# Spatial weights and six blocks of rows turned by VectorE instead of TensorE

## The chip, the core and the metric

The kernel runs on one core of a Trainium2 chip. The metric is the device time of one execution in microseconds (us). The core's engines run side by side, each through a list of instructions of its own, and wait for each other by semaphores: TensorE (PE in the profile, its weight loads PEld) multiplies and writes to PSUM; VectorE (DVE) and ScalarE (ACT) compute element by element; GpSimd (POOL) does a little arithmetic and issues transfers; SyncE (SP) issues transfers only.

## The reference

It is one inference step of a decoder layer. 256 prompt rows and 8 sample rows, each 2048 wide, all in float32, go through two sub-layers. The first has three token mixers side by side:

```python
h = rmsnorm(x, g_pre_mix) * (1.0 + sc1) + sh1          # sh, sc, gt: silu(c) @ w_ada + b_ada, in six parts
z = h @ w_in                                           # 2048 -> 15376, split into the branches' inputs
y_a = u * (einsum('gnm,bcmge->bcnge', w_s * tril, v) + b_s)   # A: spatial gating, w_s is 8 groups of 128x128
y_b, y_c = ...                                         # B: HGRN2 recurrence, C: GLA recurrence
merged = sum_n sigmoid(z_gate[n]) * (y_n @ w_branch[n])
out = merged @ w_out                                   # the output projection, 2048 -> 2048
x = x + gt1 * rmsnorm(out, g_post_mix)
h2 = rmsnorm(x, g_pre_mlp) * (1.0 + sc2) + sh2
y2 = square(relu(h2 @ w_mlp_up)) @ w_mlp_down          # 2048 -> 8192 -> 2048
x = x + gt2 * rmsnorm(y2, g_post_mlp)
```

The outputs are x for prompt and samples, the recurrent states, and the normalised v rows of the samples.

## The kernel before, in words

**Layout.** Activations lie with the features on the 128 partitions and the 264 rows (256 prompt, 8 sample) along the free axis, so that a product reads a 128x128 piece of a weight as the stationary operand and 264 columns as the moving one. A weight is loaded in float32 and split in two parts of a faster 32-bit type, `whi` (a cast by ScalarE, L673) and `wlo` (the rest, by VectorE, L677); the activations are split in the same manner, and a product is three matmuls: hi x hi, hi x lo, lo x hi.

**Granules.** The unit of work is a granule: four 128-row steps of a weight by 256 columns, which is one load of 512 KB on SP's queue, two halves to split on ScalarE and VectorE, and 24 matmuls. `Stream` loads weights five granules ahead (`LOAD_AHEAD`) and splits them two ahead (`SPLIT_AHEAD`). `linear` strings the granules of one 256-column block together (four for 2048 input rows, two for 1024) and calls `background` after each. `background` counts granules in `now`, runs what was put in `later` for an earlier count (an entry made at count n runs when `now` has passed n), and lets the generators of the mixers take steps.

**Stages.** First the input projection of the parts for branches A and B, in five chunks of the 2048 input rows (`CHUNKS`), while the first two parts of the conditioning (`First`) are made chunk by chunk; in the fourth chunk the tables for branch A are loaded (`const_a`, L907, one every other granule). Then the mixers, run as generators between granules of the remaining input projection, the gates and the branch projections; then the output projection, eight blocks of four granules; a short stage of norms; the MLP in eight slices of 1024 hidden features, each an up-projection and, one slice later, a down-projection of eight blocks of two granules; and a tail with the last norm and the residual.

**Order.** TensorE's order is the order of the code throughout. In the first stage all engines' orders are; in the mixers GpSimd's too; in the output projection and the MLP only TensorE's, while VectorE's, ScalarE's, SP's and GpSimd's orders are laid out by a planner with durations of its own. An engine waits in order: an instruction whose operand isn't there holds all behind it.

**Turning by TensorE.** A block of the output projection and of the last down-projection has features on partitions; the residual needs rows on partitions. `gated` scales a block into `g` (VectorE and ScalarE), `to_tokens` turns it by four TensorE transposes (L96), and `put_rows` (L1659, L1660) copies it out of PSUM. For the output projection `products` (L1652) and `squares` (L1656) make two sums per row, from which the next norm is known without another pass. This is done one granule after the block's end, through `later`. The spatial weights are turned by eight transposes in `mixer_a`, and masked by `triu` on their way out of PSUM.

**Turning by VectorE.** `Rows` does this elsewhere in the kernel already (v of the mixers, their keys and their outputs). `V.transpose` (L850) turns 32x32 blocks in place of one 128x128; `out` (L853) writes the 512 KB tile to DRAM (`rows_d`) on GpSimd's queue; `back` (L859) reads it again in four pieces on the same queue, so that the blocks come to their partitions; a copy puts the columns in order.

**Conditioning.** The other four of six parts are made by `Rounds`: a round is 1 MB of `w_ada` in two tiles (L379) and four matmuls of 512 columns (`ada` in the profile). A batch of rounds is due once `ADA_LAND` = 4 granules have passed since its last load. `slot` puts the mixers' small products in between granules, and counts TensorE's instructions (`T.n`) to see whether there is room for them. During the output projection six rounds of the last part are loaded ahead into spare tiles (`pre`, two at each block of `PRE_AT`). There are 28 such tiles (`blk`), shared by all stages.

Of the kernel before, what the change touches and what calls it, by code (L numbers as in the profile page):

```python
# [7 lines left out]
F32 = mybir.dt.float32  # L8
# [7 lines left out]
P = 128  # L16
# [28 lines left out]
ST_BUFS = 4  # L45
VB_BUFS = 2
N_PRE = 6
PRE_AT = (2, 3, 4)
ADA_BATCH = (4, 8)
ADA_LEAD = 3  # L50
PAIRED = 72
# [21 lines left out]
def hybrid_step_kernel(  # L73
# [288 lines left out]
    class Rounds:  # L362
# [2 lines left out]

        def __init__(self):
            self.todo, self.ws, self.done, self.at = [], [], None, 0
            self.pace, self.batch, self.gap = 5, 1, 0

        def load(self, place=None):  # L370
            r, k = self.todo.pop(0)
# [17 lines left out]

        def due(self):  # L390
            if self.ws:
                return self.full() and now[0] >= self.at + ADA_LAND
            return self.done is not None and not self.todo and now[0] >= self.at + 2 * ADA_LAND

        def tick(self):
# [435 lines left out]
        return linear(win, 0, KT, c0, width, hH, hL)  # L831


    rows_d = dp.tile([13, P, 1024], F32, tag="rows_d", name="rows_d")
    n_turned = [0]

    class Rows:
# [67 lines left out]
    def const_a(src):  # L905
        consts_a.append(blk([P, 8, P]))
        nc.sync.dma_start(consts_a[-1], src)  # L907

    srcs_a = [
        sgu_ln_g[0].partition_broadcast(P).rearrange("p (g n) -> p g n", g=8),  # L910
        sgu_ln_b[0].partition_broadcast(P).rearrange("p (g n) -> p g n", g=8),
        sgu_w_s[0].rearrange("g n m -> n g m"),
        sgu_b_s[0].rearrange("g n -> (g n)").partition_broadcast(P).rearrange("p (g n) -> p g n", g=8),
    ]
    def to_tokens(vt):
# [30 lines left out]


    def mixer_a():
        lng, lnb, wsr, bsb = consts_a
        lng, lnb = (v.rearrange("p g n -> p (g n)") for v in (lng, lnb))  # L950
        vr, vtk = rows_a.rows, []
        wsT = blk([P, 8, P])
        w00 = tmp([P, 8], "w00", 1)
        for gg in range(2):
            ps = sm()
            for i in range(4):
                T.transpose(ps[:, i * P:(i + 1) * P], wsr[:, 4 * gg + i, :], ident)
            yield
            mul(wsT[:, 4 * gg:4 * gg + 4, :], ps.rearrange("p (g n) -> p g n", g=4), triu.unsqueeze(1).to_broadcast([P, 4, P]))
        yield  # L960
        vs = tmp([P, 8, NS], "vsa", 1)
        w8 = tmp([P, 8, NS], "vsb", 1)
# [140 lines left out]
    for ci, n in enumerate(CHUNKS):  # L1103
# [5 lines left out]
        for gi in range(ng):  # L1109
# [35 lines left out]
            if final:  # L1145
                if gi in (6, 12, 18):
                    rounds.steps()
                if gi in (0, 2, 6, 8, 12, 14, 18):
                    rounds.load()
                if gi in (6, 7, 8, 9):  # L1150
                    rows_a.half((gi - 6) // 2, gi % 2)
                if gi in (8, 10):
                    rows_a.out(gi // 2 - 4)
                if gi in (11, 13):
                    rows_a.back((gi - 11) // 2)
                now[0] += 1
                if gi >= 12:
                    bg.pump(1.0)
            if ci == len(CHUNKS) - 2 and gi >= 11:
                if gi == 11:  # L1160
                    nc.sync.dma_start(cst[:, 256:904], consts[:, 256:904])
                    nc.sync.dma_start(msk, masks.rearrange("p (l t) -> p l t", l=6))
                elif gi % 2 == 0:
                    const_a(srcs_a.pop(0))
# [438 lines left out]
    branch(0, parts_a)  # L1603
    gates_b = gate_tiles(5120)
    narrow[1] = False
    branch(1, lambda: parts_b(gates_b))
    rate[:] = RATES[2]
    rounds.pace, rounds.batch, rounds.gap = 4, 4, 0
# [41 lines left out]
    def products(m, t, g, pt):  # L1650

        V.scalar_tensor_tensor(g[:, 1, 0:CW].rearrange("p (m f) -> p m f", m=2), in_rows(x1, t, m), 1.0, pt[:, t], ALU.mult, ALU.mult,  # L1652
                               accum_out=sums[:, 0, t, m:m + 1])

    def squares(m, t, g, pt):
        S.activation(g[:, 0, 0:CW].rearrange("p (m f) -> p m f", m=2), pt[:, t], AF.Square, accum_out=sums[:, 1, t, m:m + 1])  # L1656

    def put_rows(m, pt, rows):
        S.copy(in_rows(rows, 0, m), pt[:, 0])  # L1659
# [2 lines left out]
    def block_rows(m, g):  # L1662

        pt = to_tokens(g)
        for t in range(2):
            products(m, t, g, pt)
        put_rows(m, pt, og)
        for t in range(2):
            squares(m, t, g, pt)

    def norms(meanwhile):

# [12 lines left out]
    mH, mL = tiles(mh), tiles(ml)  # L1685

    sums = tmp([P, 2, 2, NS], "fs")
    pre = Rounds()
    pre.todo = [(5, k) for k in range(KT)]
    for m in range(8):  # L1690
        if m in PRE_AT:
            n = N_PRE // len(PRE_AT)
            for _ in range(n):
                pre.load(True)
        z = linear(w_out[0], 0, KT, m * CW, CW, mH, mL)
        if m < 7:
            g = gated(m, z, G1)
            later.append((now[0], lambda m=m, g=g: block_rows(m, g)))
        if m == 6:

            S.activation(tmp([P, 1], "srr", 1), sqacc[:, 0:1], AF.Sqrt)
    rounds.drain()
    rounds = pre
    A2 = A1
# [33 lines left out]
        products(7, t, g, pt)  # L1738
    both = xx3[:, 0:2]
    V.reduce_sum(both[:, :, 2:2 + NS], ps.rearrange("p s k b -> p s b k"), axis=mybir.AxisListType.X)  # L1740
    V.reduce_sum(both[:, :, 0:2], sums, axis=mybir.AxisListType.X)
    rounds.steps(3)

    d1 = tmp([P, 2, P], "vt")
# [111 lines left out]
    def down(f, ah, al):  # L1856
        for m in range(8):
# [7 lines left out]
                add(dst, dst, z)  # L1865
            if f == NFB - 1:
                g = gated(m, dst, G2)
                later.append((now[0], lambda m=m, g=g: put_rows(m, to_tokens(g), yt)))

    zs = begin_up()  # L1870
    order.__exit__(None, None, None)
# [3 lines left out]
    for f in range(NFB):  # L1875
        nxt = up(f + 1) if f + 1 < NFB else None
        if f == NFB - 1:
            rounds.drain()
            mul(G2, mod[:, 5 * KT:6 * KT, :], gpost2T.unsqueeze(2).to_broadcast([P, KT, NC]))
            yt = [[blk([P, 1024]) for _ in range(2)] for _ in range(2)]  # L1880
        last = pend
        down(f, *pend)
        pend = nxt
# [150 lines left out]
```

## Time and profile before

| | |
|---|---|
| median of 3 runs | 1782.7 us |
| the three runs | 1784.19, 1778.4, 1782.7 us |
| profiled execution | 1779.23 us |
| its span | 1777.4 us |
| TensorE matmul busy | 1756.2 us, 99% of the span, 16866 instructions |
| VectorE, ScalarE, GpSimd busy | 67%, 56%, 10% |
| granted TensorE clock, mean | 0.999 of full speed |
| moved by DMA | 455.67 MB, mean 256 GB/s |

The span goes from the first to the last instruction of the profiled execution; its own time has a little around the span. Busy shares are means over stages. The chain of waits goes back from the last instruction, at each step to what released it, so that what stands in it with its length is what set the end. In a row of the chain the first number is the start, the second the length in us; `sm L96` are transposes by TensorE, `mm L92` the products of granules, `ada L92` the conditioning. In a row of a window come its length, then busy time and count of PE, PEld, DVE, ACT and POOL, the granted clock, the mean busy share of the 16 DMA engines and GB/s.

### The profile page before, as it was taken

Reading aid. Unit: us, or ns where it says so; the run is one execution under the profiler, and the core shown is the slowest. Engines: PE = TensorE matmul, PEld = TensorE weight load, DVE = VectorE, ACT = ScalarE, POOL = GpSimd, SP = SyncE. Lnnn points to the kernel's source line nnn. Section 1 sums busy time; section 2 is a strip of 40 time slices with the busy share of each in tenths; the row PEclk is TensorE's granted clock in tenths of the full one; section 3 lists DMA queues with packets and bytes.
Section 4 is the critical chain, followed back from the end, with each engine's and each line's share of the span. In section 5 each row is a group of like instructions: output and inputs, shape, how many; then the busy total and the mean of one; then the engine's idle time right before and its main releaser. Section 6 shows DMA issues by size and latency. Waiting matters only on the chain.

```text
span 1777.4 us, 42031 instructions
## 1 busy us (share of the span) xinstructions
PE 1756.2 (99%) x16866; PEld 1675.6 (94%) x16866; DVE 1191.9 (67%) x2094; ACT 997.0 (56%) x1810; POOL 175.6 (10%) x293
## 2 busy tenths in 40 slices
PE   7999999999999999999999999999999999999998
PEld 5899999999999989899999989999999999999997
DVE  5676679887786885566666666645666666666666
ACT  5444456667777666445555666555454545454554
POOL 4222010122121122300000010000000000000000
PEclk9999999999999999999999999999999999999999
DMA  9998699899989899998667847786666666666663
GB/s 348 400 351 303 218 328 302 258 333 310 330 282 320 291 353 327 381 304 274 201 199 230 293 125 238 235 270 189 193 198 194 197 196 194 198 194 198 192 195 114
DMA packets 334547, 455.67 MB, mean 256 GB/s; under 512 B 15986, under 2 KB 277984, under 8 KB 334352
## 3 DMA queue, kind: packets, MB, share of 16 engines
q1 hardware_dynamic: 312160, 381.05, 66.3%
q0 software_dynamic: 21552, 71.48, 11.5%
q8 instruction: 132, 2.16, 0.5%
q14 instruction: 63, 0.52, 0.1%
q10 hardware_dynamic: 640, 0.47, 0.1%
HBM read 434.42 MB, written 18.51 MB: 255 GB/s over the span
## 4 chain that ended last, share of the span: by engine, by line
PE 96%; DMA 1%; DVE 1%; SPq 0%; ACT 0%; issue 0%; DVEq 0%; ACTq 0%
PE mm L92 87%; PE ada L92 5%; PE sm L92 3%; PE sm L96 1%; DMA raw<-in_w_in_dram 1%; DMA b<-in_x_prompt_dram 0%; DMA b<-in_w_ada_dram 0%; DVE wlo L677 0%; SPq L537 0%; DVE b L142 0%; DVE b L1774 0%; ACT b L148 0%; DVE b L145 0%; DVE b L139 0%; SPq L189 0%
## 5 line engine op out<-in xcount | busy, mean ns | idle before, releaser
L92 PE MATMUL mm<-b,whi 128*128 128x264 f32 x9248 | 1577.4, 277 | 1.0 <-DVE b L142 0.5
L92 PEld LDWEIGHTS mm<-b,whi 128*128 128x128 f32 x9248 | 1394.4, 189 | 34.6 <-issue 16.5
L92 PE MATMUL mm<-b,wlo 128*128 128x264 f32 x4624 | 1275.7, 276 | 0.2 <-DVE wlo L677 0.2
L677 DVE TENSOR_TENSOR wlo<-raw,whi 128x512 fp32r<-128x512 f32 x1118 | 758.4, 689 | 425.1 <-ACT whi L673 417.5
L673 ACT CAST whi<-raw 128x512 fp32r<-128x512 f32 x1118 | 679.7, 616 | 634.0 <-DVE wlo L677 320.8
L92 PEld LDWEIGHTS mm<-b,wlo 128*128 128x128 f32 x4624 | 873.5, 189 | 0.7 <-DVE wlo L677 0.4
L142 DVE TENSOR_TENSOR b<-b,mm 128x528 f32<-128x528 f32 (+1 forms) x137 | 95.7, 699 | 72.7 <-PE mm L92 66.3
L1964 POOL TENSOR_TENSOR gs<-b,G 128x16 f32<-128x16 f32 x1 | 0.2, 222 | 714.1 <-DVE b L142 714.1
L92 PE MATMUL ada<-b,cT 128*32 128x256 f32 (+2 forms) x880 | 64.8, 420 | 2.4 <-DMA b<-in_w_ada_dram 2.1
L92 PEld LDWEIGHTS ada<-b,cT 128*32 128x32 f32 x880 | 26.1, 112 | 31.0 <-issue 15.9
L537 POOL DMA_DIRECT2D b<-in_w_ada_dram x64 | 46.3, 726 | 43.8 <-PE ada L92 33.5
L1307 POOL DMA_DIRECT2D out_dram<-st x32 | 23.5, 736 | 209.5 <-DVE st L1306 207.2
L673 ACT CAST whi<-araw 128x512 fp32r<-128x512 f32 x38 | 23.2, 619 | 28.8 <-PE mm L92 25.2
L92 PE MATMUL ada<-araw,cT 128*32 128x512 f32 x272 | 36.9, 598 | 0.0
L139 DVE TENSOR_TENSOR b<-b,b 128x512 f32<-128x512 f32 (+1 forms) x49 | 34.5, 719 | 2.5 <-ACT b L1416 0.8
L1304 ACT ACTIVATE st<-st,fs 128x128 f32<-128x128 f32 (+1 forms) x96 | 35.1, 427 | 0.0
L1306 DVE SCALAR_TENSOR_TENSOR st<-vbc,b,st 128x128 f32<-128x128 f32 (+1 forms) x96 | 32.2, 390 | 2.3 <-DMA vbc<-vs_d 1.7
L859 POOL DMA_DIRECT2D b<-rows_d x52 | 28.6, 556 | 27.4 <-ACT whi L673 7.2
L677 DVE TENSOR_TENSOR wlo<-araw,whi 128x512 fp32r<-128x512 f32 x38 | 24.5, 685 | 1.3 <-ACT whi L673 1.3
L145 DVE TENSOR_TENSOR b<-gt,b 128x528 fp32r<-128x528 f32 x32 | 22.8, 713 | 3.2
L145 DVE TENSOR_TENSOR b<-b 128x1024 f32<-128x1024 f32 (+1 forms) x24 | 24.4, 1019 | 0.1
L92 PE MATMUL sm<-b,b 128*32 128x32 f32 (+2 forms) x320 | 22.9, 237 | 0.7 <-DVE b L139 0.7
(308 smaller groups left out, 826.1 us busy)
## 6 DMA issues: line engine op xcount, KB each, us to landing
raw<-in_w_in_dram SPq DMA_DIRECT2D x225, 512.0 KB, 5.7
raw<-in_w_mlp_down_dram SPq DMA_DIRECT2D x128, 512.0 KB, 3.6
raw<-in_w_mlp_up_dram SPq DMA_DIRECT2D x125, 512.0 KB, 3.9
araw<-in_w_ada_dram SPq DMA_DIRECT2D x68, 512.0 KB, 6.7
b<-in_w_ada_dram SPq DMA_DIRECT2D x60, 512.0 KB, 6.8
b<-in_w_ada_dram POOLq DMA_DIRECT2D x48, 512.0 KB, 9.5
raw<-in_w_branch_dram SPq DMA_DIRECT2D x48, 512.0 KB, 5.6
raw<-in_w_out_dram SPq DMA_DIRECT2D x32, 512.0 KB, 4.3
```

The source lines that it names most:

```text
L92: return nc.tensor.matmul(out, w, x, **kw)
L96: return nc.tensor.transpose(*a)
L139: V.tensor_tensor(o, a, b, op=ALU.mult)
L142: V.tensor_tensor(o, a, b, op=ALU.add)
L145: V.tensor_tensor(o, a, b, op=ALU.subtract)
L537: queue.dma_start(w[:, i], w1[k * P:(k + 1) * P, :, self.k0 * P:(self.k0 + self.n) * P])
L673: self.last = [S.copy(hi, raw).ins, None]
L677: self.last[1] = V.tensor_tensor(lo, raw, hi.bitcast(F32), op=ALU.subtract).ins
L859: nc.gpsimd.dma_start(t[32 * q:32 * q + 32, :].rearrange("p (s c) -> p s c", s=4), rows_d[self.d0 + i].rearrange("(s p) (q c) -> q p s c", ...
L1304: S.activation(st[:, i, :], st[:, i, :], AF.Copy, scale=fs[:, h0 + i, b:b + 1])
L1306: V.scalar_tensor_tensor(st[:, i, :], v[:, i, :], k[:, h0 + i, NP + b:NP + b + 1], st[:, i, :], ALU.mult, ALU.add)
L1307: nc.gpsimd.dma_start(G.s_out(b, h0, nh), st)
```

## The change

Three groups of transposes go from TensorE to VectorE by way of `Rows`: the spatial weights; the first two of the output projection's eight blocks, as one pair; and the first four of the last down-projection's, as two pairs. A pair's two blocks are turned into one tile (`put`), written out, read back one granule later (`back`), and copied into the rows after 5 (output projection) or 2 (down-projection) further granules (`natural`), each step run by `later` one count after the one named. The pair's sums at the output projection are then made over 512 columns at once (`block_sums`), so `sums` has seven columns in place of eight. The spatial weights are turned in the first two granules of the fifth chunk, read back at the fifth, and masked straight from there.

For this the four tables and two constants of branch A are loaded four granules earlier, the spatial weights first; the last two of the six rounds loaded ahead go from the output projection's fifth block (number 4) to its sixth; and from the second branch projection on, a batch of rounds is due after five granules in place of four.

```diff
-PRE_AT = (2, 3, 4)
+PRE_AT = (2, 3, 5)
...
-            self.pace, self.batch, self.gap = 5, 1, 0
+            self.pace, self.batch, self.gap, self.land = 5, 1, 0, ADA_LAND
...
-                return self.full() and now[0] >= self.at + ADA_LAND
+                return self.full() and now[0] >= self.at + self.land
...
-    rows_d = dp.tile([13, P, 1024], F32, tag="rows_d", name="rows_d")
+    rows_d = dp.tile([19, P, 1024], F32, tag="rows_d", name="rows_d")
...
     srcs_a = [
+        sgu_w_s[0].rearrange("g n m -> n g m"),
         sgu_ln_g[0].partition_broadcast(P).rearrange("p (g n) -> p g n", g=8),
         sgu_ln_b[0].partition_broadcast(P).rearrange("p (g n) -> p g n", g=8),
-        sgu_w_s[0].rearrange("g n m -> n g m"),
...
         for gg in range(2):
-            ps = sm()
-            for i in range(4):
-                T.transpose(ps[:, i * P:(i + 1) * P], wsr[:, 4 * gg + i, :], ident)
+            mul(
+                wsT[:, 4 * gg:4 * gg + 4, :].rearrange("p k (s f) -> p k s f", s=4),
+                rows_w.rows[0][:, gg],
+                triu.rearrange("p (s f) -> p s f", s=4).unsqueeze(1).to_broadcast([P, 4, 4, 32]),
+            )
             yield
-            mul(wsT[:, 4 * gg:4 * gg + 4, :], ps.rearrange("p (g n) -> p g n", g=4), triu.unsqueeze(1).to_broadcast([P, 4, P]))
...
+                if gi == 0:
+                    rows_w = Rows(consts_a[0:1], lambda b, r: b[:, 4 * r:4 * r + 4, :].rearrange("p k (q f) -> p k q f", q=4))
+                if gi < 2:
+                    rows_w.half(0, gi)
+                if gi == 1:
+                    rows_w.out(0)
+                if gi == 4:
+                    rows_w.back(0)
...
-            if ci == len(CHUNKS) - 2 and gi >= 11:
-                if gi == 11:
+            if ci == len(CHUNKS) - 2 and 7 <= gi < 16:
+                if gi == 7:
...
+    rounds.land = ADA_LAND + 1
     branch(1, lambda: parts_b(gates_b))
...
+    class Pairs:
+        def put(self, m, g):
+            i = m % 2
+            if i == 0:
+                self.r = Rows([None])
+                self.r.ts[0] = blk([P, 1024])
+            to = self.r.ts[0].rearrange("p (q r k f) -> p r k q f", q=4, r=2, k=4)
+            for t in range(2):
+                V.transpose(to[:, t, 2 * i:2 * i + 2], g[:, :, t * P:(t + 1) * P].rearrange("p k (q f) -> p k q f", q=4))
+            if i:
+                self.r.out(0)
+                self.soon(1, self.back, m // 2, self.r)
+        def soon(self, n, f, *a):
+            later.append((now[0] + n, lambda: f(*a)))
+            later.sort(key=lambda x: x[0])
+        def back(self, b, r):
+            r.back(0)
+            self.soon(self.landed, self.natural, b, r.rows.pop())
+        def natural(self, b, v):
+            w = slice(b % 2 * 512, b % 2 * 512 + 512)
+            for t in range(2):
+                (V.tensor_copy if t else S.copy)(self.rows[t][b // 2][:, w].rearrange("p (k s f) -> p k s f", k=4, s=4), v[:, t])
+            self.then(b, w)
+    def block_sums(b, w):
+        for t in range(2):
+            junk = tmp([P, 512], "gt")
+            y = og[t][b // 2][:, w]
+            V.scalar_tensor_tensor(junk, x1[t][b // 2][:, w], 1.0, y, ALU.mult, ALU.mult, accum_out=sums[:, 0, t, b:b + 1])
+            S.activation(tmp([P, 512], "vt"), y, AF.Square, accum_out=sums[:, 1, t, b:b + 1])
...
+    pairs = Pairs(og, 5, block_sums)
...
-            later.append((now[0], lambda m=m, g=g: block_rows(m, g)))
+            later.append((now[0], lambda m=m, g=g: block_rows(m, g) if m > 1 else pairs.put(m, g)))
...
-                later.append((now[0], lambda m=m, g=g: put_rows(m, to_tokens(g), yt)))
+                later.append((now[0], lambda m=m, g=g: put_rows(m, to_tokens(g), yt) if m > 3 else pairs.put(m, g)))
...
+            pairs = Pairs(yt, 2, lambda b, w: None)
```

More of the change, by code (lines that the diff above doesn't have):

```diff
@@ L948, in mixer_a @@
     def mixer_a():
-        lng, lnb, wsr, bsb = consts_a
+        _, lng, lnb, bsb = consts_a
         lng, lnb = (v.rearrange("p g n -> p (g n)") for v in (lng, lnb))
@@ L1652, in products @@
         V.scalar_tensor_tensor(g[:, 1, 0:CW].rearrange("p (m f) -> p m f", m=2), in_rows(x1, t, m), 1.0, pt[:, t], ALU.mult, ALU.mult,
-                               accum_out=sums[:, 0, t, m:m + 1])
+                               accum_out=sums[:, 0, t, m - 1:m])
     def squares(m, t, g, pt):
-        S.activation(g[:, 0, 0:CW].rearrange("p (m f) -> p m f", m=2), pt[:, t], AF.Square, accum_out=sums[:, 1, t, m:m + 1])
+        S.activation(g[:, 0, 0:CW].rearrange("p (m f) -> p m f", m=2), pt[:, t], AF.Square, accum_out=sums[:, 1, t, m - 1:m])
     def put_rows(m, pt, rows):
@@ L1669, in block_rows, with __init__ @@
             squares(m, t, g, pt)
+    class Pairs:
+        def __init__(self, rows, landed, then):
+            self.rows, self.landed, self.then = rows, landed, then
+        def put(self, m, g):
[26 more added lines that the diff above has]
+            S.activation(tmp([P, 512], "vt"), y, AF.Square, accum_out=sums[:, 1, t, b:b + 1])
     def norms(meanwhile):
@@ L1697, in hybrid_step_kernel @@
             g = gated(m, z, G1)
-            later.append((now[0], lambda m=m, g=g: block_rows(m, g)))
+            later.append((now[0], lambda m=m, g=g: block_rows(m, g) if m > 1 else pairs.put(m, g)))
         if m == 6:
             S.activation(tmp([P, 1], "srr", 1), sqacc[:, 0:1], AF.Sqrt)
+    assert not later
     rounds.drain()
@@ L1740, in hybrid_step_kernel @@
     V.reduce_sum(both[:, :, 2:2 + NS], ps.rearrange("p s k b -> p s b k"), axis=mybir.AxisListType.X)
-    V.reduce_sum(both[:, :, 0:2], sums, axis=mybir.AxisListType.X)
+    V.reduce_sum(both[:, :, 0:2], sums[:, :, :, 0:7], axis=mybir.AxisListType.X)
     rounds.steps(3)
```

## The prediction

> **What bounds the kernel now.** I read the page's busy shares first, then what TensorE waited for, then the chain of waits around each place of the change.
>
> ```profile
> span 1777.4 us, 42031 instructions
> PE 1756.2 (99%) x16866; PEld 1675.6 (94%) x16866; DVE 1191.9 (67%) x2094; ACT 997.0 (56%) x1810; POOL 175.6 (10%) x293
> ```
>
> TensorE leaves 21.2 us of the span unused. The same question to the waits of TensorE, from 85 to 1040 us, which holds all stages between the start and the end of the output projection:
>
> ```profile
> engine line waited for: us in total, times, longest us
> PE sm L92 <- DVE b L139: 0.7, 1, 0.7
> PE mm L92 <- DVE b L142: 0.5, 3, 0.2
> PE mm L92 <- DVE wlo L677: 0.2, 1, 0.2
> ```
>
> So 1.4 us in 955 are waits; the rest is TensorE working in its written order. Whatever leaves that order shortens the span, and a load that comes sooner can at most win those 1.4 us. Now the chain around the three places, start and length in us: the spatial weights (first six rows), two blocks of the output projection, two blocks of the last down-projection.
>
> ```profile
> 260.75 0.59 PE sm L96 x4
> 261.33 2.70 PE mm L92 x24
> 264.04 0.44 PE sm L96 x4
> 264.47 10.80 PE mm L92 x96
> 278.20 1.85 PE ada L92 x16
> 280.05 8.30 PE mm L92 x72
> ...
> 964.68 10.80 PE mm L92 x96
> 975.49 0.44 PE sm L96 x4
> 975.92 10.80 PE mm L92 x96
> ...
> 1726.71 5.40 PE mm L92 x48
> 1732.12 0.44 PE sm L96 x4
> 1732.55 5.40 PE mm L92 x48
> ```
>
> A granule of 24 products takes 2.70, and every set of four transposes stands bare between two granules: nothing overlaps it.
>
> **Removed from TensorE.** Output projection: block to block is 975.92 - 964.68 = 11.24, of which 10.80 are products, so one set costs 0.44; two blocks, 0.88. Down-projection: 1732.55 - 1726.71 = 5.84 less 5.40, again 0.44; four blocks, 1.76. Spatial weights: the second set is 0.44. The first follows an ada batch, behind which products lose time anyway: 280.05 has 8.30 for 72, 0.20 more than 3 x 2.70. So it costs 0.59 - 0.20 = 0.39, and the two sets 0.83. **Sum 0.88 + 1.76 + 0.83 = 3.47 us.** 32 transposes, nothing else leaves the path.
>
> **Added on VectorE and ScalarE.** Two transposes of 256 elements in `put` for each of the six blocks, twelve in all, and two of 512 for the spatial weights; per pair of blocks one copy of 512 on each engine, and at the output projection the sums over 512 instead of over two times 256.
>
> ```profile
> L850 DVE STREAM_TRANSPOSE b<-b x26: 668/704/712, 242.5 to 700.8; 128x512 f32<-128x512 f32 x26
> L1660 DVE COPY b<-sm x14: 416/418/424, 967.3 to 1761.6; 128x256 f32<-128x256 f32 x14
> L1462 ACT COPY b<-b x3: 614/619/620, 433.4 to 686.3; 128x512 f32<-128x512 f32 x3
> L1462 DVE COPY b<-b x3: 422/428/428, 434.5 to 686.4; 128x512 f32<-128x512 f32 x3
> 1724.00:1754.00 30.00, 30.00 (x270) 30.00 (x269) 24.15 (x51) 18.96 (x37) 0.00 (x0) 1.00 0.50 153
> 964.00:975.00 11.00, 11.00 (x101) 11.00 (x100) 7.05 (x17) 6.79 (x15) 0.00 (x0) 1.00 0.90 306
> ```
>
> In the windows' rows VectorE is the fourth number, ScalarE the fifth. A transpose of 256 is not in the trace: it lies between 0.35 (half of 0.70) and 0.70 (no shorter for half); I take 0.42, what a copy of that size takes. The last down-projection is the tight place: VectorE is busy 24.15 of 30, or 4.70 of a block's 5.84. Afterwards a block has 5.40, and VectorE 4.70 - 0.42 + 2 x 0.42 = 5.12 (4.98 to 5.68 by the bounds), and once per pair 0.43 more: 5.55 in that block. What hides an excess: the weights of a granule are split two granules ahead (SPLIT_AHEAD), 2 x 2.70 = 5.40. By the dear bound four blocks run over by 0.28 each and two by 0.43, 1.98 in all, still under 5.40. At the output projection 7.05 of 11 leaves room. ScalarE gives up two copies (0.37) for one (0.62). Cost: 0; without that cover it would be the 1.98.
>
> **Added transfers.** Each of the four turned tiles goes out to DRAM and comes back as four pieces, on POOL's queue, which no one else uses in these stages.
>
> ```profile
> L859 POOL DMA_DIRECT2D b<-rows_d x52: 550/552/589, 254.3 to 729.0; - x52
> L853 POOL DMA_DIRECT2D rows_d<-b x13: 544/559/598, 248.3 to 705.0; - x13
>   ACT b L1462: 1.7, 2
>   DVE b L1462: 1.1, 2
> DMA to landing us min/median/max: 3.6/6.9/10.0
> ```
>
> Write, then reads: 6.9 + 3 x 0.55 + 6.9 = 15.5 at the median, 21.7 at the longest. The copies behind a read wait for it in order on ScalarE and VectorE. In the program's order the copy stands 1 + 1 + 1 + 5 = 8 granules (21.6 us) behind `put` at the output projection and 5 (13.5) in the last down-projection; so 0 late there, 2.0 late here (8.2 at the longest). What is queued behind it is the next splits, and TensorE would wait for these, with 5.40 of lead: 0 at the median, 2.8 per pair at the longest. I take 0: DMA runs at half share there (0.50 in the row above), whereas these 6.9 come from full stages. Spatial weights: the read is issued eight granules (21.6) ahead of its first use; 0.
>
> [...]
>
> **Moved loads.** The four tables for branch A are issued four granules (10.8 us) earlier in the fourth chunk.
>
> ```profile
> 180.00:185.00 5.00, 5.00 (x47) 5.00 (x46) 3.79 (x6) 2.33 (x4) 0.00 (x0) 1.00 0.18 69
> 195.00:200.00 5.00, 5.00 (x47) 5.00 (x46) 2.33 (x6) 2.60 (x5) 1.35 (x4) 1.00 0.00 0
> 215.00:220.00 5.00, 5.00 (x46) 5.00 (x46) 3.58 (x7) 2.37 (x4) 0.00 (x0) 1.00 0.89 292
> 975.00:986.00 11.00, 11.00 (x100) 11.00 (x99) 7.41 (x18) 6.60 (x16) 0.00 (x0) 1.00 1.02 361
> 1009.00:1020.00 11.00, 11.00 (x100) 11.00 (x100) 7.40 (x18) 6.83 (x15) 0.00 (x0) 1.00 0.61 193
> ```
>
> The last two numbers are DMA share and GB/s. The new places, about 185 to 206, hold idle stretches (0.18, 0.00); the old one was at 0.89, and takes the spatial weights' trip instead. SP waits for weights' buffers as before. The last ada preload moves from the fifth to the sixth block, out of 1.02 towards 0.61, and must be there at 1040, some 30 us on, against 13.4 for the slowest such load below. Cost 0, gain at most the 1.4 us of waits.
>
> ```profile
> 821.36 1.85 PE ada L92 x16
> 1040.22 1.85 PE ada L92 x16
> DMA to landing us min/median/max: 3.7/6.7/13.4
> ```
>
> The last row is of the ada loads in rounds. Five granules instead of four before a batch counts as landed is 13.5 instead of 10.8 us; batches end later, but the last one before the projection ends at 823, 130 us before anything needs it. Fewer TensorE instructions also shift when a slot has room for the small products of the mixers; bounds: the waits of 0.7 and 0.2 above go, or as much comes. I take 0.
>
> **Against which time.** The profiled execution took 1779.23, 1.83 more than its span; the sum gives 1775.8. The median of the three runs is 1782.7, 3.47 higher (by chance the same figure as the sum), which gives 1779.2. The four executions average 1781.1; less 3.47, **1777.7**, minus 0.2%. This kernel's runs can't tell less than 0.3% (5.3 us) from nothing, so the likeliest verdict is no difference. Its own range is 0.9 beyond both bases: 1774.9 to 1780.1.
>
> **Rivals.**
> *Late transfers vanish too* (20%). The slowest run is 5.0 us above the profiled one. If late loads make that (ada loads of 13.4 us against an allowance of 10.8; DMA shares over 1), the spread loads bring all runs down to 1779.23 - 3.47 = 1775.8, 6.9 under the median: faster. Against: the profiled run shows no wait of TensorE for a load after 85 us.
> *The copies wait in place of TensorE* (12%), the slower side. VectorE's and ScalarE's order is a planner's in both stages, so a copy may stand right behind the reads' issue: 3 x 0.55 + 6.9 = 8.55 late, less 5.40 of lead, 3.15 for each of three pairs, 9.45, net +6.0: 1787.1; with landings of 10.0, 18.8, net +15.3. It decides once each copy waits longer than 5.40 + 3.47 / 3 = 6.6 us. For it: copies of L1462 did wait for such reads. Against: 1.7 and 1.1 us in two times each.
> *VectorE becomes the bound of the last down-projection* (8%): blocks stay at 5.84, the 1.76 are lost: 1779.4, no difference. It needs transposes far above 0.70.
>
> [...]
>
> **How the numbers follow.** Forecast 60%, rivals 20, 12 and 8. The range reaches to the first rival with the runs' spread (1771) and short of the second (1786). Faster: the first rival and 6% of the forecast's, 0.26; slower: most of the second, 0.10; same 0.64.
>
> **What would show it.** Right: no L96 set behind the first two projection blocks and the first four of the down-projection, block starts 10.80 and 5.40 apart, the span 3 to 4 us shorter, TensorE's waits about the same. Wrong: a wait of TensorE for wlo L677 or whi L673 near 1000 or 1745, with copies before it that sat idle until `b<-rows_d`; blocks that stay at 5.84; or a span more than 5 us shorter, with the gain outside these three places.

## The result, and the profile after

| | before | after |
|---|---|---|
| median of seven runs each | 1781.93 us | 1786.73 us |
| lowest and highest | 1778.4, 1785.69 us | 1783.26, 1790.2 us |
| profiled execution | 1779.23 us | 1787.2 us |
| its span | 1777.4 us | 1785.4 us |

After to before is **1.0026, with a 95% interval of 1.0014 to 1.0038**: 4.6 us slower (2.5 to 6.8), where 1777.7 had been forecast, a little faster. The change lies within the 0.3% that the prediction called no difference, but its sign is clear, and the time is 0.7 above the top of the range (1786).

The two profiled executions are 8.0 apart in their spans, more than the medians, because each is one draw from its spread. The page of the changed kernel begins:

```profile
span 1785.4 us, 42033 instructions
PE 1760.8 (99%) x16834; PEld 1674.7 (94%) x16834; DVE 1193.7 (67%) x2101; ACT 997.1 (56%) x1803; POOL 186.5 (10%) x313
```

The 32 transposes are gone (16866 to 16834), yet TensorE's busy time rose by 4.6 us: some products ran at half the clock (from 245.8 to 249.2 us the granted clock was 0.50, and they started 220 ns apart instead of 113), and conditioning products that a wait tears apart show more busy time (four by themselves 1.05 us in the rows below, sixteen in a row 1.85). And it waits at new places. Its waits from 24 to 1790 us, in the columns of the prediction's table (total, times, longest):

```profile
PE ada L92 <- DMA b<-in_w_ada_dram: 3.3, 2, 2.1
PE sm L96 <- ACT gt L1647: 1.1, 1, 1.1
PE sm L92 <- DVE st L1315: 0.5, 1, 0.5
```

The first row is conditioning products that stand in TensorE's order before their weights have landed. The kernel before has one such wait over the same stretch:

```profile
PE ada L92 <- DMA b<-in_w_ada_dram: 1.8, 1, 1.8
```

But it lies before 85 us, in the start; the prediction's table, from 85 to 1040, has none. The two of the changed kernel come at 244 and 756 us.

If TensorE's time is summed between the same products in both traces, the 8.0 fall into stages like this (us, after less before; worked out from the starts of all its instructions):

| stage | difference | of it |
|---|---|---|
| start, to 90 us | -0.4 | |
| fifth chunk of the first projection | +5.1 | ada +4.3, slower products +1.6, transposes gone -0.8 |
| mixers and branch projections, 290 to 960 | +4.2 | ada +2.5, other small products +2.0, the rest less |
| output projection | +0.4 | two sets gone -0.88, then +1.3 |
| last down-projection | -1.8 | |
| sum | +7.5 | the other 0.5 lies behind the last products |

The row of the mixers alone proves little. Each trace is one execution, and that of the kernel before was a quick one there: nine of the experiments below have TensorE's products in the order of before up to 960 us, and in the same row their traces have 0.3 to 7.7 us more than it. What a moved order costs is read from the runs' times.

**Fifth chunk.** Windows of the changed kernel, then of the kernel before (length, then PE, PEld, DVE, ACT, POOL busy with counts, granted clock, DMA share, GB/s):

```profile
240.00:245.00 5.00, 2.93 (x19) 0.53 (x17) 2.53 (x4) 1.50 (x3) 0.00 (x0) 1.00 1.04 302
245.00:250.00 5.00, 5.00 (x28) 4.66 (x27) 0.00 (x0) 0.67 (x2) 0.00 (x0) 0.66 1.01 388
250.00:255.00 5.00, 5.00 (x47) 5.00 (x47) 4.82 (x8) 4.06 (x6) 0.56 (x1) 1.00 0.28 104
```
```profile
235.00:240.00 5.00, 5.00 (x47) 5.00 (x46) 3.82 (x6) 3.57 (x6) 0.00 (x0) 1.00 1.02 381
240.00:245.00 5.00, 5.00 (x44) 3.44 (x43) 2.53 (x4) 1.88 (x3) 0.00 (x0) 1.00 0.61 187
```

Before, the DMA engines are full until about 240 (a share of 1.02) and then have room (0.61); TensorE never stops. After, they are full ten microseconds longer (1.04 and 1.01), TensorE idles for 2 us of the first window, and in the second it starts 28 matmuls instead of 47 although it shows as busy throughout: the granted clock is 0.66 there. The chain of the changed kernel says for what it stood still:

```profile
232.96 11.35 DMA b<-in_w_ada_dram
...
244.36 1.05 PE ada L92 x4
```

This load was issued at 232.96, and landed at 244.31. In the kernel before, the same one was issued at 232.81 and landed at 239.78, 6.97 later. Between the two lies GpSimd's read of the turned spatial weights, issued from 235.16 to 236.80 and landed up to 244.14. From the batch's first product to the next product of a weight it is 5.1 us, instead of 1.85. In all five traces with the trip in this chunk the batch is longer, 2.6 to 5.1; in the twelve others it is 1.85.

**Mixers.** The chain near 750:

```profile
739.73 16.70 DMA b<-in_w_ada_dram
...
756.47 1.05 PE ada L92 x4
```

Before, the sixteen products of this batch stand in a row:

```profile
749.89 1.72 PE ada L92 x16
```

**Output projection.** The transposes from 960 to 1012 us, before and after (count, shortest, median and longest in ns, first and last start):

```profile
L96 PE MATMUL sm<-cst,gt x20: 272/273/273, 964.1 to 1009.4; 128*128 128x128 f32 x20
```
```profile
L96 PE MATMUL sm<-cst,gt x8: 272/272/328, 1005.4 to 1007.5; 128*128 128x128 f32 x8
```

Before, every block's set stands bare with 0.44 behind 10.80 of products. After, the first two blocks' sets are gone, and the third block's comes a block late, right in front of the fourth's. This is a side effect of the change: `background` looks at the first entry of `later` only, and the third block's entry is appended behind that of the pair's copies, which is due later. The fourth block's set then waits:

```profile
993.36 10.43 DMA raw<-in_w_out_dram
...
1006.66 0.39 ACT gt L1647
...
1007.09 0.66 PE sm L96 x4
```

A weight took 10.43 to land (the median of such loads was 4.3 before); the splits behind it came late on ScalarE, `gt` stood behind them and behind the pair's squares (L1720) in ScalarE's order, and the transposes of `gt` waited 1.1. The two copies of the pair also sat idle for their read (from 960 to 1012 us):

```profile
ACT b L1711 <- DMA b<-rows_d: 4.4, 1, 4.4
DVE b L1711 <- DMA b<-rows_d: 3.7, 1, 3.7
```

But they ran at 999.8, four us before that weight landed, and are not on the chain.

**Last down-projection.** The chain has 355 products in one piece without a transpose, where before there was a set every 48:

```profile
1719.95 39.94 PE mm L92 x355
1759.88 0.44 PE sm L96 x4
```

39.94 / 355 x 48 is 5.40 for a block, so the blocks start 5.40 apart, and the whole 1.8 us arrive.

### The profile page after: what moved, and what is told of

It reads as the page before. It is cut to its first block, busy times and chain, and to the rows that moved or that the text cites. A ratio compares the mean times of both kernels' runs of the same rounds, so it can differ in the third digit from the quotient of the medians.

```text
span 1785.4 us, 42033 instructions
## 1 busy us (share of the span) xinstructions
PE 1760.8 (99%) x16834; PEld 1674.7 (94%) x16834; DVE 1193.7 (67%) x2101; ACT 997.1 (56%) x1803; POOL 186.5 (10%) x313
## 4 chain that ended last, share of the span: by engine, by line
PE 95%; DMA 3%; DVE 1%; ACT 1%; SPq 0%; issue 0%; DVEq 0%; ACTq 0%
PE mm L92 85%; PE ada L92 5%; PE sm L92 3%; DMA b<-in_w_ada_dram 2%; PE sm L96 1%; DMA raw<-in_w_out_dram 1%; DMA b<-in_x_prompt_dram 0%; DVE wlo L677 0%; DVE b L1827 0%; DVE b L142 0%; ACT whi L673 0%; ACT b L148 0%; DVE b L145 0%; SPq L537 0%; SPq L189 0%
## 5 line engine op out<-in xcount | busy, mean ns | idle before, releaser
L853 POOL DMA_DIRECT2D rows_d<-b x17 | 9.5, 561 | 861.8 <-DVE b L1694 786.8
L92 PE MATMUL ada<-b,cT 128*32 128x256 f32 (+2 forms) x888 | 69.1, 428 | 5.1 <-DMA b<-in_w_ada_dram 5.0
L859 POOL DMA_DIRECT2D b<-rows_d x68 | 37.4, 556 | 50.2 <-DMA rows_d<-b 16.6
L1901 ACT ACTIVATE b<-vt 128x528 fp32r<-128x528 f32 x32 | 23.1, 720 | 1.0
```

Source lines behind the costliest of these rows:

```text
L92: return nc.tensor.matmul(out, w, x, **kw)
L859: nc.gpsimd.dma_start(t[32 * q:32 * q + 32, :].rearrange("p (s c) -> p s c", s=4), rows_d[self.d0 + i].rearrange("(s p) (q c) -> q p s c", ...
L1901: S.activation(apart(a), by_two(rl), AF.Square)
```

## The experiments

The theory after the result: the time that TensorE saves is as forecast; it is lost to two things, the spatial weights' trip, which makes a conditioning load late, and a moved order of the mixers, which makes another one late. The rivals: the copies behind the reads; the due time of five granules; a spread that hides a gain.

The measured times of all fifteen, against runs of the kernel before on the same chip (a ratio where there were several runs; else the single time and the median beside it):

| kernel | time, us | to before, interval |
|---|---|---|
| s_only: spatial weights alone | 1787.13 | 1.0031 [1.002, 1.0042] |
| s_count: the same, order kept | 1784.31 | 1.0015 [1.0006, 1.0024] |
| count_only: the order alone | 1785.83 | 1.0023 [1.0014, 1.0032] |
| count_half: half the shift | 1781.56 | 0.9997 [0.9988, 1.0006] |
| count_plus: shift the other way | 1787.36 | 1.0029 [1.0018, 1.004] |
| s_early: trip in the fourth chunk, order kept | 1782.96 | 1.0011 [1.0001, 1.0022] |
| l_only: due time alone | 1781.48 | 1.0002 [0.9992, 1.0013] |
| no_land: whole change, due time back | 1787.84 | 1.003 [1.0019, 1.0042] |
| land4_order: no_land, order kept | 1784.41 | 1.0015 [1.0005, 1.0025] |
| d_only: last down-projection alone | 1780.71 | 0.9998 [0.9986, 1.0009] |
| o_only: output projection alone | 1780.95 | beside 1781.02 |
| o_held: its copies held back | 1783.98 | beside 1781.02 |
| o_late: and its loads ahead later | 1780.78 | beside 1781.72 |
| do_late: both sorts of blocks, as in o_late | 1781.0 | 0.9999 [0.999, 1.0008] |
| best: whole change, order kept, trip early, copies held | 1782.1 | 1.0003 [0.9992, 1.0014] |

### The spatial weights, with and without the order

`s_only` is the kernel before with the spatial weights' part of the change and its moved tables. `s_count` adds one line where a set of four transposes was, so that `slot` finds the same count as before:

```diff
             mul(wsT[:, 4 * gg:4 * gg + 4, :]..., rows_w.rows[0][:, gg], triu...)
+            T.n += 8
             yield
```

> As s_count, but the eight transposes are no longer counted, so slots find room at other granules and the mixers' products stand in another order (24 of 60 places differ). Theory (the order is part of the mixers' loss of 5.1 us): 1 to 4 us more than s_count, with TensorE's waits between 590 and 900. Rival (the mixers' loss is the later due time of the rounds alone): equal to s_count within 1 us.

> The kernel before with the spatial weights' part alone (turned by VectorE, tables loaded four granules earlier), and with the eight removed transposes still counted in T.n, so that the mixers' small products stand between the same granules as before. Theory (the read of the turned weights collides with the ada load of the fifth chunk's third granule, which TensorE must have at the sixth): TensorE waits 2 to 4 us in an ada batch near 240, the granted clock halves after it, the fifth chunk is 4 to 6 us longer, the rest unchanged: time +4 to +5 us. Rival (the wait in the profile after was a chance of that execution): no wait over 0.5 us near 240, time -0.8 us. Rival (the loss sits in the mixers' order alone): also -0.8.

Both are slower, by 5.5 us (0.0031 x 1782; 3.6 to 7.5) and by 2.7 (1.1 to 4.3). So the trip with its moved tables, and nothing else in the order moved, costs more than its two sets save; and the other 2.8 came with the order. The wait that `s_count` expected is there, but the clock did not fall behind it, and the 4 to 5 us of its theory are missed. The profile of `s_count`, its waits from 85 to 1040 us:

```profile
PE mm L92 <- ACT gt L1559: 3.3, 2, 1.8
PE ada L92 <- DMA b<-in_w_ada_dram: 1.3, 1, 1.3
```

The second is the collision of the fifth chunk: there TensorE's conditioning takes 3.44 more and the transposes 0.77 less, +2.6 in the stage, about the whole of the median's difference. The first lies in the mixers, at 739 and 760 us, and is of the kind that changes from run to run (below).

### The order alone

```diff
                 T.transpose(ps[:, i * P:(i + 1) * P], wsr[:, 4 * gg + i, :], ident)
+            T.n -= 8
```

The kernel before with only its counter changed by what the transposes counted: nothing is computed or moved otherwise.

> The kernel before, all transposes still on TensorE, but eight of them are not counted in T.n, so the mixers' products stand in the order of s_only. Theory (the order alone costs what s_only has over s_count, 2.8 us): +2 to +4 us, all of it between 590 and 900, waits of TensorE there. Rival (the order is harmless; s_only's excess came from the fifth chunk): within 1 us of before.

It costs **4.1 us (2.5 to 5.7)**: almost as much as the whole change. Its waits and its chain near 750:

```profile
PE ada L92 <- DMA b<-in_w_ada_dram: 3.7, 2, 2.5
```
```profile
740.26 14.14 DMA b<-in_w_ada_dram
...
754.45 1.05 PE ada L92 x4
```

The batch that stalled in the changed kernel stalls here too, with all transposes still on TensorE: its load took 14.14. In the kernel before, the batch's last load was issued 2.4 us earlier, at 737.82, took 11.29, and landed 1.0 before the first product that needs it. The four traces in which the transposes aren't counted (after, s_only, count_only, no_land) all stall at this batch: from its first product to the next product of a weight it is 4.8 to 6.8 us, instead of 1.83; of the traces with the order of before none does. The DMA engines are full here: from 740 to 755 the share is 1.03 to 1.05 in both count_only and the kernel before.

That the order costs is shown by the times. Where the 4.1 sits is shown in part: these four traces lack a wait at about 549 us which all others have (0.6 to 3.0, see below), so the stall isn't the whole account.

Two more, to see whether it is any shift or this batch:

> The kernel before with its count of TensorE's instructions lowered by 4 per group instead of 8: nothing is computed otherwise, and the order differs at 3 of 76 places, all near the start of the mixers' products, instead of at 24. If the cost of the moved order sits in the later places (the ada batch near 750), this is 0 within 0.001 and has no wait there. If any shift of the count costs because it moves the first products of the mixers, it is near 1.0023 as with 8.

> The kernel before with its count of TensorE's instructions raised by 8 per group: nothing is computed otherwise, and the order differs at 14 of 76 places. If the written order is simply the best one near it, this costs too: 1.001 to 1.003. If what costs is one collision (the loads of the ada batch near 750 issued late because the order puts them behind a tile that is still in use), this has no wait there, and lies within 0.001 of 1, or below.

With half the shift (`T.n -= 4`) only the places near the start of the mixers move, and it costs nothing: 0.9997. With the shift turned round (`T.n += 8`) it costs 5.2 us (3.2 to 7.1), as its first theory expected and against the second's nothing; the trace has the same kind of wait at another place:

```profile
722.60 16.40 DMA b<-in_w_ada_dram
...
739.04 1.92 PE ada L92 x4
```

Another batch, 17 us earlier, is reached before its loads. TensorE waited 5.2 us for one that was issued at 721.31 and landed at 736.72, and then 0.4 for this one, which took 16.40. So it isn't one bad place: the loads that were waited for in this stretch took 12 to 17 us, and an order that moves a batch against its loads can run into one. Last, the old order put back under the whole change (with the due time of four granules, since five moves the batches as well):

> The changed kernel with the due time back at four granules, so its mixers' order is that of s_only. Theory (the order by count costs, the due time doesn't): within 1.5 us of the changed kernel's 1.0026, that is +3 to +6 us. Rival (the later due time pays for itself in the changed order, or costs): 2 us and more above or below the changed kernel.

> The changed kernel with the due time back at four granules and the count of TensorE's instructions raised by 8 per group, so that the mixers' small products stand where the kernel before has them (56 of 60 places from the fifth chunk's end on, and the other four are places of transposes that left TensorE). If the order alone costs about 4 us (1.0023 when it was moved by itself), the same change without this was 1.003 and this is near 1.0007: between 1.0 and 1.0014, with no wait of ada products near 750. If the stall near 750 comes from the transfers that the change adds and not from the order, the ratio stays near 1.003 and the wait is there.

The ratio goes from 1.003 to 1.0015, so the order is worth about 2.7 us here (the two intervals overlap), and the wait at 750 is gone. What stays is a little more than expected (1.0014 at most). The batch of the fifth chunk still takes 3.5 us instead of 1.85, since the trip is still there. Its longest waits:

```profile
PE sm L92 <- DVE b L139: 3.0, 1, 3.0
PE sm L96 <- ACT gt L1647: 1.7, 1, 1.7
```

The second is the output projection's. The first stands at about 549, in every trace that has before's order, and is 0.6 (o_late), 0.7 (before), 1.0 (s_early), 2.1 (d_only), 2.3 (do_late) and 3.0 (o_held and here) long: a draw of the run, with the same products in the same order. Those of TensorE behind `gt` between 735 and 760 are drawn likewise, from 0 to 3.3 in total. Together they could make 5.7 (2.4 + 3.3) of the 7 us by which the runs of one kernel differ; this is an estimate, as no kernel was traced twice.

### The trip moved to the fourth chunk

`s_early` is `s_count` with the spatial weights turned in granules 13 and 14 of the fourth chunk, written out at 14 and read back at 17, about 203 to 220 us. In the changed kernel, which has its tables moved likewise, the DMA share is 0.78 from 203 to 210 and 0.88 from 210 to 220; from 229 to 244 it is 0.89 in the kernel before and 1.02 with the trip there.

```diff
-                if gi < 2:
-                    rows_w.half(0, gi)
...
+            if ci == len(CHUNKS) - 2:
+                if gi in (13, 14):
+                    rows_w.half(0, gi - 13)
+                if gi == 14:
+                    rows_w.out(0)
+                if gi == 17:
+                    rows_w.back(0)
```

> As s_count, but the spatial weights are turned, written and read back in the fourth chunk (granules 13 to 17, about 203 to 220 us) instead of the fifth. Theory (the read collides with the ada load of the fifth chunk): no wait of TensorE in the ada batches of the fifth chunk over 0.4 us, the chunk 0.8 us shorter than before, time -0.8 us, so 3 to 4 us under s_count. Rival (the tables' earlier loads, or the turning as such, cost it): time as s_count, about +2.7.

1.0011 (1.0001 to 1.0022): the batch at 240 no longer waits, but no gain comes. The chain shows the next batch but one:

```profile
276.12 2.87 PE ada L92 x16
```

It takes 2.87 where it took 1.85 before. TensorE came 0.83 earlier, and the batch took 1.02 more: its load, it seems, came when it came. The stage ends 0.2 later than before. So the 0.83 of the spatial weights was not to be had here (the last experiment, `best`, shows the same): where it came free, the next batch but one took longer. What makes the median 1.9 above before's I can't place: this profiled execution was the fastest of its runs (1778.65), and its fifth chunk and mixers take just 0.2 and 0.3 more than in before's trace.

### The due time

```diff
+    rounds.land = ADA_LAND + 1
     branch(1, lambda: parts_b(gates_b))
```

> The kernel before with the due time alone: five granules in place of four from the second branch projection on. Theory (batches that are due later meet fewer of the mixers' slots and their loads queue up): +1 to +4 us between 600 and 900, nothing elsewhere. Rival (only the count of instructions matters, or DMA chance): within 1 us of the kernel before in its profile's mixers stage.

Nothing: 1.0002. Taking it out of the whole change (no_land) doesn't help either.

### The last down-projection

> The kernel before with the last down-projection's four blocks alone turned by VectorE. Theory: block starts 5.40 apart instead of 5.84 for four blocks, span -1.8 us and no wait of TensorE for splits there, everything up to 1720 as before. Rival (copies waiting for the read hold up the splits or the tail): 5.84 stays or the tail is longer by 1 us and more, time not shorter.

The edit is the change's line `put_rows(...) if m > 3 else pairs.put(m, g)` with its `Pairs`, and nothing else. The chain:

```profile
1719.96 32.40 PE mm L92 x288
1752.36 0.44 PE sm L96 x4
```

Six blocks in 32.40, 5.40 each, and the stage is 1.80 shorter than before, as forecast. Yet the span is again 1777.4, and the ratio 0.9998: this run's mixers took 3.1 us more than before's trace, 1.4 of it in the wait at 549.

```profile
PE sm L92 <- DVE b L139: 2.1, 1, 2.1
```

### The output projection

`o_only` is the pair of blocks with its sums and `PRE_AT = (2, 3, 5)`. `o_held` also holds the copies behind splits that stand eight or more casts further on ScalarE:

```diff
-            for t in range(2):
-                (V.tensor_copy if t else S.copy)(...)
+            with tc.issue_after(stream[0].last[0]), tc.issue_after(stream[0].last[1]):
+                for t in range(2):
+                    (V.tensor_copy if t else S.copy)(...)
```

> The kernel before with the output projection's first pair alone turned by VectorE (and the ada preload moved from the fifth to the sixth block). Read by the span from the output projection's start to its end. Theory (ScalarE and VectorE stand behind the copies, which the planner put right behind the reads' issue): two sets of 0.44 gone, one wait of TensorE of about 1.1 us behind ScalarE near 1005, net +0.2 to +0.5 us, the copies idle for 3 us and more until b<-rows_d. Rival (that wait in the profile after was chance): -0.88 us, no wait.

> As o_only, but the two copies are held behind the weight splits that the code has issued by then, so the planner can't put them earlier (they stand eight casts later on ScalarE). Theory: the copies no longer wait for the read, no wait of TensorE near 1005, the output projection 0.88 us shorter than before. Rival (the transfers themselves delay the weights' loads): the wait of TensorE stays at 0.5 us or more.

In `o_only` the stage has 0.88 less and then 1.6 more. With the copies held, 0.88 less and 0.9 more: the gain is just given back. The wait for `gt` is there in both, and the chain of `o_held` shows that the copies aren't its cause:

```profile
989.08 10.31 DMA raw<-in_w_out_dram
...
1001.86 0.48 ACT gt L1637
...
1002.39 0.66 PE sm L96 x4
```

A weight's load of 10.31 again. From 985 to 1000 the DMA share is 1.03 to 1.08: the pair's 1 MB of trip is under way there beside the weights and the conditioning loaded ahead. In the kernel before no weight of this stage took over 7.0, in the traces with the pair the longest took 8.1 to 11.6. So the next ones move these ahead loads to blocks 4, 5 and 6:

> As o_held, but the six ada preloads go to the fifth, sixth and seventh block of the output projection, out of the way of the pair's trip (third to fourth block). Theory (the trip's 1 MB on top of two blocks' preloads makes a w_out load land 10 us late, and ScalarE and VectorE stand behind its cast): no w_out load over 8 us, no wait of TensorE for gt, the output projection 0.88 us shorter than before. Rival (the trip alone delays the load): the wait for gt stays, 0.5 us or more.

> The last down-projection's four blocks and the output projection's pair turned by VectorE, copies held behind the splits, preloads in the fifth to seventh block; the spatial weights stay with TensorE. Theory: TensorE's time after the branch projections 2.6 us shorter than before (0.88 + 1.76), time -2 to -2.6 us, ratio 0.9985 to 0.999. Rival (the gain of the output projection is given back at the next load, as in the fifth chunk): -1.8 us or less, ratio 0.999 or more.

In `o_late` the wait was still there (1.2): the planner of SP's order issued four of these loads at 980 to 989 all the same, beside the trip's reads. In `do_late`, the same code with the down-projection's blocks added, it did so too (981 to 990), but no load of `w_out` took over 8.1, and:

```profile
984.92 13.72 PE mm L92 x122
998.65 0.87 PE sm L96 x8
999.52 10.80 PE mm L92 x96
```

No wait, with the third and the fourth block's sets in one row here too: so the moved set alone doesn't make the wait. After the branch projections this run has 2.7 us less than before (0.88 + 1.81), all that the two sorts of blocks can give. Between a load of 8.1 and one of 10.0 lies the whole difference. Even so the ratio is 0.9999 (0.999 to 1.0008): 2.7 of 1781 is 0.0015, just outside the interval, and I can't show it in the runs' times. Whether holding SP's ahead loads away from the trip would make it sure was not tried, nor was the third block's set put back in its place.

### All of it with what was learnt

> All three groups turned by VectorE as in the change, but with the spatial weights' trip in the fourth chunk, the eight transposes still counted in T.n, the copies held behind the splits and the due time left at four granules. Theory (the 3.47 us of transposes are real, and collision, order and early copies ate them): TensorE's time outside the mixers 3.3 to 3.6 us shorter than before, time -3 to -3.5 us, ratio 0.998. Rival (something else of the change costs the time too): ratio 0.9995 or more.

1.0003. The fifth chunk now costs 0.24, the end gives its 1.81, the order is before's (yet this execution, the slowest of its twelve runs, has 7.7 more than before's trace in the mixers, with 5.4 of waits and two falls of the clock); the output projection gives its gain back and 1.3 more, with the longest load of `w_out` in any trace:

```profile
991.43 11.61 DMA raw<-in_w_out_dram
```

So no version beats the kernel before by more than the runs can tell.

## Why the prediction was wrong

**What held.** TensorE's terms: the down-projection gave 1.80 of 1.76 in every trace; the two sets that left the output projection took 0.88 along until the wait gave it back. VectorE isn't the bound of the last down-projection (that rival is dead: blocks 5.40 apart). The due time is worth 0, as taken. In the last down-projection the copies cost 0, as taken, though one pair's sat idle there for 2.3 and 1.4 us.

**The failed step: "Fewer TensorE instructions also shift when a slot has room for the small products of the mixers; [...] I take 0."** Its bounds were 0.9 down and "as much" up; measured alone it is +4.1 (2.5 to 5.7), more than the whole saving of 3.47. The prediction looked at what waits there were in before's order (1.4 us), and took this small sum for the size of what another order could bring. But a sum of waits says only how well this order fits. Near 750 the DMA engines are full (a share of 1.04 to 1.05 from 740 to 755); in before's order the last load of the batch landed 1.0 us before it was needed, in the four traces without the count 3.3 to 5.3 us after. How the 4.1 divides among the places stays open.

**The second: "Spatial weights: the read is issued eight granules (21.6) ahead of its first use; 0."** True of the read, which nobody waited for. The price is paid by others: a conditioning load beside it took 11.35 instead of 6.97, and it has a fixed place in TensorE's order. 2.7 net with the order kept (1.1 to 4.3), so about 3.5 of cost against 0.83 of saving. The sentence on the moved tables did see that the old place "takes the spatial weights' trip instead", but read the windows of 180 to 220, not those of 229 to 244 where the trip lies (a share of 0.89 before, 1.02 after). GpSimd's queue was free, as the prediction said, and with its read under way SP's load took 4.4 us longer all the same.

**The third: output projection, 0.88.** It came and was given back. The rival of the copies had the right place and in part the right chain (copies idle 4.4 and 3.7 us, splits late), but not the main cause: with the copies held the wait stays. A late weight load is what ends last in the chains, and TensorE waits for `gt` behind the late splits, 0.7 to 2.1 us once, not 3.15 for each of three pairs. That the trip makes that load late is argued from the kernel before, which has the ahead loads without the trip, and there no such load took over 7.0; no run has the trip without the ahead loads beside it. The prediction also left each remaining set in its place; the third block's moved.

**The sum** of the parts measured alone: 4.1 (order) + 2.7 (trip, its sets off) - 1.8 (down-projection, by its traces) + 0 (output projection, due time) = +5.0; the whole measures +4.6. The first two have intervals of 1.6 either way, so that this near an agreement is partly luck. The first rival, that the runs' spread would vanish, is wrong too: 6.9 us between lowest and highest after, 7.3 before.

## What to carry to other kernels

Here work taken off the busiest engine shortened only those stages in which that engine, and not its loads, set the pace: 1.80 us in the last down-projection (DMA share 0.50), nothing for the 0.83 of the spatial weights. So look at the DMA share around each place, and count a new transfer by how much later it makes the loads beside it that have a fixed consumer, not by when its own reader needs it. Where an order is steered by a count of instructions, an edit in one stage reorders another (by itself +4.1 us here); run that shift by itself, with nothing else changed, before crediting or blaming the edit. And few waits in a profile (1.4 us of 955 here) show that the order fits its loads, not that another order would fit as well.

## What the runs showed of the hardware that was not expected

**After a short wait the clock was halved.** After some of the waits above the granted clock falls to 0.5 for exactly 3.413 us (once for 6.827), at moments that lie a whole multiple of 3.413 us after the clock's first rise (65, 155, 157, 209 and 216 times). Products then start 220 ns apart instead of 113; in the fifth chunk of the changed kernel this added 1.6 us to the 3.3 by which the batch had become longer. Laid into this grid, windows just before a drop (after, l_only, o_held, then two of best, then count_plus):

```profile
242.41:245.82 3.41, 1.46 (x8) 0.63 (x9) 0.44 (x1) 0.00 (x0) 0.00 (x0) 1.00 1.05 353
```
```profile
547.58:550.99 3.41, 1.45 (x13) 1.28 (x12) 2.91 (x9) 2.85 (x6) 0.00 (x0) 1.00 0.72 220
```
```profile
549.16:552.57 3.41, 0.44 (x4) 0.41 (x4) 2.91 (x8) 3.08 (x7) 0.00 (x0) 1.00 0.64 196
```
```profile
547.96:551.37 3.41, 1.24 (x12) 1.07 (x10) 2.91 (x8) 2.62 (x6) 0.00 (x0) 1.00 0.82 258
756.17:759.58 3.41, 1.00 (x10) 0.81 (x8) 2.64 (x6) 2.44 (x5) 0.71 (x1) 1.00 1.07 398
```
```profile
732.80:736.22 3.42, 0.00 (x0) 0.00 (x0) 1.11 (x4) 1.61 (x4) 0.00 (x0) 1.00 1.02 284
```

And windows of the grid with a wait in them that no drop followed (do_late, land4_order, and two in a row of count_only):

```profile
548.39:551.80 3.41, 1.47 (x13) 1.50 (x14) 2.91 (x7) 2.33 (x5) 0.11 (x1) 1.00 0.87 279
```
```profile
551.18:554.59 3.41, 1.50 (x13) 1.52 (x14) 2.91 (x7) 2.32 (x5) 0.13 (x1) 1.00 0.90 295
```
```profile
748.16:751.57 3.41, 1.51 (x17) 0.42 (x16) 0.51 (x3) 0.58 (x2) 0.00 (x0) 1.00 1.03 388
751.57:754.98 3.41, 1.59 (x8) 0.29 (x8) 2.51 (x5) 1.17 (x4) 0.73 (x1) 1.00 1.06 392
```

TensorE's busy time (the second number) divides them. In the seventeen traces, from the clock's rise to the last granules, six windows of the grid have 1.46 of 3.41 or less, and a drop follows each; 28 lie between 1.47 and 2.4, and a drop follows none. So a drop followed the wait of 2.0 us at 549 in `l_only` and none the one of 2.3 in `do_late`, by where each fell in the grid; in the fifth chunk of the changed kernel the drop cost the 1.6. That the busy time decides is read off these windows; no run changed it on purpose.

**One load's time swings by a factor of two to three.** The same 512 KB for the conditioning landed after 6.97 us in one place and after 16.70 in another, with the DMA share at 1.02 in the first and up to 1.06 in the second; the weights of the output projection after 3.4 to 11.61. In these stages an estimate from the median (4.3 there) is off by more than all that the change could win.
